# A filler tile that is 96 floats longer, and with it the addresses of every MLP operand

## The chip, the cores and the metric

The kernel runs on one core of one Trainium2 chip. The metric is the device time in microseconds (us) from the first to the last instruction's work, as the runtime sees it, for one execution of the whole layer; lower is better. The time before is 1979.04 us, the median of three runs (1976.56, 1979.04, 1983.78).

## What is computed

One layer of a decoder trunk, float32, sequence 2048, width 1024. The first part mixes tokens (attention beside a short convolution) and adds the result to the residual; the second part is an MLP with a squared ReLU. The filler stands between the two, and the MLP is the part whose operands it moves.

```
h  = rms_norm(x, attn_norm_g);  z = h @ w_in                  # 1024 -> 2304 columns
q, k, v, B, C, xc = split(z)
y  = [rms_norm(swa_sink_attention(q, k, v)), rms_norm(B * conv3(C * xc))]
x  = x + y @ w_out                                            # 1024 -> 1024
hm = rms_norm(x, mlp_norm_g)
x  = x + square(relu(hm @ w_up)) @ w_down                     # 1024 -> 4096 -> 1024
```

## The kernel before, in words

**Three stages.** The mixers run first, in four chunks of 512 tokens, each a sequence of projections (accumulators `pz`, `pc_c`, `px_c`, `pb_c`), attention (`psc_b`, `ptp_b`, `po_b`) and output projection (`pout`). Then comes the first MLP product, called "up" here (accumulators `u`, line 1222), and then the second, called "down" (accumulators `d`, line 1328). The matrices of the MLP are cut into 2x2 blocks and multiplied in seven block products instead of eight (a Strassen-like scheme), so that up is 224 products of 12 matmuls and down is 56 steps of 48, which makes 2688 matmuls in each.

**Every matmul is split in three.** To keep float32 accuracy with the PE's rounded operand type (fp32r), each operand is stored as a high part and a remainder: ScalarE (ACT) casts the block, VectorE (DVE) subtracts, and TensorE (PE) does high x high, high x low and low x high into one accumulator. In the mixers this is the helper at lines 245 to 247; in up and down it is the innermost loop. All of these matmuls have a stationary operand of 128x128 and, where the text speaks of a wide matmul, a moving operand of 128x512. In the profile's names the moving operand stands first: `u<-op_x,wop` moves `op_x` past a stationary `wop`, and `d<-op_w,op_f` moves `op_w` past `op_f`.

**Where the operands lie.** A tile's address is its byte in each partition of SBUF. Three pools matter. `mlp_ops`, on the right side of SBUF, has 14 buffers of 8192 bytes, tag `op`, for the moving operand of up (`op_x`), and both operands of down (`op_w`, `op_f`); and then, behind the last of them, the tile `fill`. Since this pool is laid out up to the end of SBUF, the length of `fill` sets where the 14 buffers begin. `mlp_up`, on the left side, holds the stationary operand of up (`wop`, four buffers of 4096 bytes) and the raw weights and intermediate results of up; `mlp_down` takes its place in the down stage. The mixers' pools are given back before `mlp_ops` and `mlp_up` are opened. Inside a tile the pieces that one matmul reads are at multiples of 512 bytes from its start (128 or 512 floats in a row), so a tile's start says where all of its pieces lie, counted modulo 512. In the program before these starts are:

```
stage    moving operand, start mod 512      stationary operand, start mod 512
mixers   w_wo, w_q, h            0          at_b, yt_c, h, w_wc, w_wx, w_wb   0
up       op_x                  384          wop                               0
down     op_w                  384          op_f                            384
```

**What sets the order.** The order of up's products is written out (`seq`); three products ahead of the PE, ACT and DVE make the next `wop` from raw weights `wu` (lines 963 and 964), and up's results go out to DRAM as the blocks `fop` (line 975). In the first part of up, between its products, sixteen groups of four PE transposes (`pt_m`, line 1050) prepare the second half of the tokens. Down loads `fop` back, splits it (lines 896 to 898), and forms the weights' sums on DVE (line 1176) from raw blocks that SP's queue loads (line 1167). `fill` itself is only written once, by a memset of GpSimd (POOL) at line 1202, and nothing reads it.

Of the kernel before, what the change touches and what calls it, by code (L numbers as in the profile page):

```python
# [7 lines left out]
F32 = mybir.dt.float32  # L8
# [8 lines left out]
P = 128  # L17
# [75 lines left out]
def hymba_layer(  # L93
# [794 lines left out]
    ops = ctx.enter_context(tc.tile_pool(name="mlp_ops", bufs=1, side="right", reuse_waits="tile"))  # L888
# [309 lines left out]

    ready_x(0)

    fill = ops.tile([P, 24], F32, tag="fill", name="fill")
    nc.gpsimd.memset(fill, 0.0)
    for i in range(LEAD):
        ready_x(i)
# [163 lines left out]
```

## Time and profile before

| | |
|---|---|
| profiled execution | 1980.8 us, of which 1978.8 us from first to last instruction (the span) |
| PE busy | 1945.1 us (98%) of the span |
| DVE, ACT, POOL busy | 1189.2, 837.2, 317.2 us (60%, 42%, 16%) |
| DMA | 410.66 MB, mean 208 GB/s |
| chain that ended last | PE 93%: up (L1222) 32%, down (L1328) 31%, the rest in the mixers |

The profile names an instruction by its line, engine, operation and tiles. PE means matmuls and PEld the weight loads that go before them. A matmul's own duration (about 390 ns) overlaps with the next one's, so what a matmul costs the PE in a dense stretch is the distance from its start to the next one's start; it comes from a stretch's length divided by the number of matmuls in it. "The chain" is the work that ended last, followed back from the end; a row of it gives the start, the length, the line and the number of instructions. PEclk is the granted TensorE clock as a share of full speed.

### The profile page before, as it was taken

The numbers are of one execution on the slowest core, as the hardware profiler recorded it, in microseconds if no ns is written. First come the engines' busy times: TensorE is split into PE (matmuls) and PEld (weight loads), VectorE is DVE, ScalarE is ACT, GpSimd is POOL, SyncE is SP. The second block draws the span as 40 slices with busy tenths as digits, with TensorE's granted clock in tenths as the row PEclk, the third lists the DMA queues.
The fourth block names the chain that finished last, engine by engine and source line by source line (L and its number), as shares of the span: only waits on it lengthen the run. The fifth ranks groups of instructions, "written<-read, shape, count | busy, mean of one in ns | idle before, by whom it ended". The sixth has DMA issues, their size and how long they took to land.

```text
span 1978.8 us, 24773 instructions
## 1 busy us (share of the span) xinstructions
PE 1945.1 (98%) x9068; PEld 1608.4 (81%) x9068; DVE 1189.2 (60%) x1810; ACT 837.2 (42%) x1572; POOL 317.2 (16%) x492
## 2 busy tenths in 40 slices
PE   8999999999999989999999999999999999999999
PEld 7878887888788768888888888888888888888887
DVE  4875656446555759777778766665643434547441
ACT  4474435335334446444455544454433232232320
POOL 2332314313132310222201111011000000100000
PEclk9999999999999999999999999999999999999999
DMA  8875744464464696666665444436974447766641
GB/s 286 295 295 160 293 181 163 169 256 181 150 261 186 211 295 244 214 212 194 232 221 199 164 156 143 150 114 225 411 254 143 145 149 229 273 224 218 214 149 43
DMA packets 224057, 410.66 MB, mean 208 GB/s; under 512 B 18368, under 2 KB 134080, under 8 KB 212160
## 3 DMA queue, kind: packets, MB, share of 16 engines
q1 hardware_dynamic: 195072, 333.57, 49.6%
q0 software_dynamic: 15040, 50.34, 6.6%
q10 hardware_dynamic: 13824, 25.17, 3.4%
q8 instruction: 71, 1.16, 0.2%
q14 instruction: 50, 0.41, 0.1%
HBM read 283.20 MB, written 125.83 MB: 207 GB/s over the span
## 4 chain that ended last, share of the span: by engine, by line
PE 93%; DVE 3%; POOL 1%; ACT 1%; DMA 1%; issue 1%; SPq 0%; DVEq 0%; POOLq 0%; ACTq 0%
PE u L1222 32%; PE d L1328 31%; PE pout L245 3%; PE pout L247 3%; PE pout L246 3%; PE pz L246 2%; PE pz L245 2%; PE pz L247 2%; PE psc_b L502 1%; PE pc_c L246 1%; PE pc_c L245 1%; PE pc_c L247 1%; PE px_c L245 1%; PE px_c L247 1%; PE px_c L246 1%; PE pb_c L247 1%
## 5 line engine op out<-in xcount | busy, mean ns | idle before, releaser
L1222 PE MATMUL u<-op_x,wop 128*128 128x512 f32 x2688 | 634.0, 397 | 4.6 <-ACT wop L963 4.5
L1328 PE MATMUL d<-op_w,op_f 128*128 128x512 f32 x2688 | 609.6, 389 | 0.0
L1222 PEld LDWEIGHTS u<-op_x,wop 128*128 128x128 f32 x2688 | 505.1, 188 | 126.8 <-ACT wop L963 5.7
L1328 PEld LDWEIGHTS d<-op_w,op_f 128*128 128x128 f32 x2688 | 504.5, 188 | 104.8
L898 DVE TENSOR_TENSOR op_f<-op_f 128x1024 fp32r<-128x1024 f32 x112 | 136.7, 1224 | 237.2 <-ACT op_f L897 237.1
L897 ACT CAST op_f<-op_f 128x1024 fp32r<-128x1024 f32 x112 | 117.4, 1050 | 330.1 <-DMA op_f<-fop 327.2
L963 ACT CAST wop<-wu 128x512 fp32r<-128x512 f32 x160 | 99.0, 619 | 124.4 <-PE u L1222 118.3
L964 DVE TENSOR_TENSOR wop<-wu,wop 128x512 fp32r<-128x512 f32 x160 | 110.2, 689 | 43.3 <-ACT wop L963 27.5
L975 POOL DMA_DIRECT2D fop<-s x96 | 52.1, 542 | 486.3 <-DVE s L978 464.3
L981 DVE TENSOR_TENSOR u<-u,u 128x512 f32<-128x512 f32 x128 | 88.1, 688 | 35.6 <-PE u L1222 33.9
L898 DVE TENSOR_TENSOR op_w<-raw,op_w 128x1024 fp32r<-128x1024 f32 x56 | 68.4, 1223 | 34.1 <-ACT op_w L897 33.9
L897 ACT CAST op_w<-raw 128x1024 fp32r<-128x1024 f32 x56 | 58.7, 1049 | 58.2 <-PE d L1328 29.3
L1178 POOL DMA_DIRECT2D wds<-raw x16 | 8.6, 534 | 335.6 <-DVE raw L1176 335.6
L519 ACT ACTIVATE sc_b<-sc_b,ngm_b 128x128 f32<-128x128 f32 x128 | 49.6, 389 | 27.4 <-DVE ngm_b L516 27.4
L551 POOL TENSOR_SCALAR_AFFINE_SELECT pp_b<-pp_b 128x512 fp32r<-128x512 f32 x60 | 42.7, 725 | 111.6 <-ACT pp_b L544 73.1
L963 ACT CAST wop<-wu_s 128x512 fp32r<-128x512 f32 x64 | 39.6, 619 | 44.2 <-PE u L1222 42.6
L987 ACT ACTIVATE u<-u 128x512 f32<-128x512 f32 x64 | 40.5, 633 | 33.9 <-DVE u L981 30.9
L245 PE MATMUL pout<-w_wo,yt_c 128*128 128x512 f32 x128 | 52.8, 412 | 0.0
L247 PE MATMUL pout<-w_wo,yt_c 128*128 128x512 f32 x128 | 52.5, 410 | 0.0
L246 PE MATMUL pout<-w_wo,yt_c 128*128 128x512 f32 x128 | 51.9, 406 | 0.0
L245 PE MATMUL pout<-w_wo,at_b 128*128 128x512 f32 x128 | 50.2, 392 | 0.0
L247 PE MATMUL pout<-w_wo,at_b 128*128 128x512 f32 x128 | 50.0, 391 | 0.0
(236 smaller groups left out, 3181.1 us busy)
## 6 DMA issues: line engine op xcount, KB each, us to landing
op_f<-fop SPq DMA_DIRECT2D x112, 512.0 KB, 3.8
raw<-in_w_down_dram SPq DMA_DIRECT2D x72, 512.0 KB, 4.3
wu<-in_w_up_dram SPq DMA_DIRECT2D x128, 256.0 KB, 3.6
w_wo<-wo SPq DMA_DIRECT2D x24, 1024.0 KB, 6.7
fop<-s POOLq DMA_DIRECT2D x96, 256.0 KB, 2.4
fop<-u ACTq DMA_DIRECT2D x64, 256.0 KB, 2.2
op_x<-xop SPq DMA_DIRECT2D x28, 512.0 KB, 5.8
w_q<-qkv SPq DMA_DIRECT2D x24, 512.0 KB, 5.4
```

The costliest lines, as they stand in the source:

```text
L245: nc.tensor.matmul(ps, st(0), mv(0), start=first, stop=False)
L246: nc.tensor.matmul(ps, st(0), mv(1), start=False, stop=False)
L247: nc.tensor.matmul(ps, st(1), mv(0), start=False, stop=last)
L519: nc.scalar.activation(sc[:, hd, :], sc[:, hd, :], AF.Exp, bias=ngm[:, hd : hd + 1], accum_out=den[:, hd : hd + 1])
L897: nc.scalar.copy(op[:, 0], raw)
L898: nc.vector.tensor_tensor(op[:, 1], raw, op[:, 0].bitcast(F32), op=ALU.subtract)
L963: nc.scalar.copy(hi, blk)
L964: nc.vector.tensor_tensor(lo, blk, hi.bitcast(F32), op=ALU.subtract)
L975: eng.dma_start(fop_dram[tb][ORDER_DOWN.index(i)][n // 2][:, n % 2], b)
L981: nc.vector.tensor_tensor(dst, ps, b, op=ALU.add)
L1222: nc.tensor.matmul(pt, wops[i][:, a, k, :], xops[tb, p][k // 2][:, b, k % 2, :], start=p not in GOES_ON and k + j == 0, stop=k + j == NB + ...
L1328: nc.tensor.matmul(ps[tb][j], fs[tb][:, a, k, j * P : (j + 1) * P], w[:, b, k, :], start=first and p not in GOES_ON and k + n == 0, stop=l ...
```

## The change

The filler grows from 24 to 120 floats in each partition, from 96 to 480 bytes.

```diff
-    fill = ops.tile([P, 24], F32, tag="fill", name="fill")
+    fill = ops.tile([P, 120], F32, tag="fill", name="fill")
     nc.gpsimd.memset(fill, 0.0)
```

In the built program one instruction differs, the memset, which now writes 120 elements of each partition; every other instruction, its place on its engine and its waits are the same, so there is no order to show. What moves is the address of the 14 `op` buffers, by 384 bytes downwards: the first starts at 114176 instead of 114560, which is 0 instead of 384 modulo 512. The nearest tile below them ends at 113152. So the table of starts becomes 0 and 0 in up and 0 and 0 in down; the mixers keep theirs.

## Rows read from the trace of the kernel before

**Rows 1.** The page: the granted TensorE clock in 40 slices of the span, in tenths of full speed, and the two MLP products among the costliest groups (busy us, mean ns of one | idle before).

```profile
PEclk9999999999999999999999999999999999999999
...
L1222 PE MATMUL u<-op_x,wop 128*128 128x512 f32 x2688 | 634.0, 397 | 4.6 <-ACT wop L963 4.5
L1328 PE MATMUL d<-op_w,op_f 128*128 128x512 f32 x2688 | 609.6, 389 | 0.0
```

**Rows 2.** The chain that ended last, from the start of up to the start of down, in two answers (start us, length us, what): the first rows of up, and the rest of up with the beginning of down.

```profile
729.93 74.34 PE u L1222 x310
804.27 0.44 PE pt_m L1050 x4
804.70 5.59 PE u L1222 x24
810.29 0.44 PE pt_m L1050 x4
810.73 5.60 PE u L1222 x24
...
961.96 0.44 PE pt_m L1050 x4
962.40 397.59 PE u L1222 x1704
1359.99 0.24 PE d L1328
1360.22 0.06 issue
1360.29 5.82 PE u L1222 x24
1366.10 34.03 PE d L1328 x150
```

**Rows 3.** Busy time by stretch for the matmuls of down alone (line 1328): the whole of the down stage.

```profile
core 0: us, PE busy (x) PEld busy (x), PEclk, DMA share, GB/s
...
1366.00:1975.00 609.00, 609.00 (x2687) 504.07 (x2686) 1.00 0.60 207
```

**Rows 4.** Busy time by stretch for the matmuls of up alone (line 1222).

```profile
740.00:800.00 60.00, 60.00 (x260) 48.66 (x259) 1.00 0.71 249
...
804.00:965.00 161.00, 157.92 (x662) 122.90 (x661) 1.00 0.64 205
965.00:1360.00 395.00, 394.99 (x1693) 317.43 (x1691) 1.00 0.51 172
```

**Rows 5.** Timeline of the PE in two settled stretches of the mixers, the first and the last matmul of each (start us, duration us). The first stretch has 80 wide matmuls, the second 82, one to a row.

```profile
213.04 0.39 PE L245 MATMUL pout<-w_wo,at_b 128*128 128x512 f32 x1
...
230.95 0.39 PE L246 MATMUL pc_c<-h_h,w_wc 128*128 128x512 f32 x1
...
390.42 0.39 PE L246 MATMUL pout<-w_wo,at_b 128*128 128x512 f32 x1
...
408.78 0.39 PE L246 MATMUL pc_c<-h_h,w_wc 128*128 128x512 f32 x1
```

**Rows 6.** Timeline of the PE in the mixers just behind an interruption by narrower matmuls.

```profile
252.38 2.08 PE L502 MATMUL psc_b<-kw,qt_b 128*128 128x256 f32 x16
254.29 0.40 PE L245 MATMUL px_c<-h_h,w_wx 128*128 128x512 f32 x1
254.53 0.40 PE L246 MATMUL px_c<-h_h,w_wx 128*128 128x512 f32 x1
254.76 0.39 PE L247 MATMUL px_c<-h_h,w_wx 128*128 128x512 f32 x1
254.99 0.40 PE L245 MATMUL px_c<-h_h,w_wx 128*128 128x512 f32 x1
255.22 0.39 PE L246 MATMUL px_c<-h_h,w_wx 128*128 128x512 f32 x1
255.46 0.39 PE L247 MATMUL px_c<-h_h,w_wx 128*128 128x512 f32 x1
```

**Rows 7.** Busy time by stretch of all engines, over up and, in the second part, over two settled stretches of the mixers.

```profile
core 0: us, PE busy (x) PEld busy (x) DVE busy (x) ACT busy (x) POOL busy (x), PEclk, DMA share, GB/s
729.00:804.00 75.00, 74.92 (x312) 60.11 (x312) 65.39 (x95) 46.00 (x70) 6.87 (x18) 0.96 0.77 266
804.00:965.00 161.00, 161.00 (x726) 130.24 (x725) 121.91 (x177) 76.32 (x127) 39.45 (x45) 1.00 0.64 205
965.00:1360.00 395.00, 395.00 (x1694) 317.62 (x1692) 284.86 (x421) 209.63 (x340) 47.53 (x86) 1.00 0.51 172
...
213.00:231.00 18.00, 18.00 (x81) 14.89 (x81) 11.47 (x22) 4.06 (x7) 9.14 (x14) 1.00 0.79 309
235.00:252.00 17.00, 17.00 (x77) 14.07 (x76) 8.45 (x17) 5.93 (x24) 0.18 (x1) 1.00 0.92 356
```

**Rows 8.** Waits: those of the PE over the whole of up (729 to 1366 us), then the longest of the other engines for the PE between 965 and 1360 us, then one of SP's queue between 1300 and 1420 us (who waited <- for whom: us in total, times, longest).

```profile
PE u L1222 <- ACT wop L963: 4.5, 1, 4.5
...
ACT wop L963 <- PE u L1222: 100.0, 78, 2.2
...
SPq L1167 <- DMA fop<-u: 21.1, 1, 21.1
```

**Rows 9.** Timeline of DVE where the third step of down gets its operand `op_f` (two blocks, one for each half of the tokens).

```profile
1385.77 2.35 DVE L898 TENSOR_TENSOR op_f<-op_f 128x1024 fp32r<-128x1024 f32 x2
```

**Rows 10.** The same work of DVE at either offset (mean ns of one behind the busy time): the split of `op_f`, at 384 modulo 512, and the difference of two raw weight blocks, at 0; and the DMA issues of 512 KB into `op_f` and into `raw_t` (x count, KB, median us to landing), with the same two offsets.

```profile
L898 DVE TENSOR_TENSOR op_f<-op_f 128x1024 fp32r<-128x1024 f32 x112 | 136.7, 1224 | 237.2 <-ACT op_f L897 237.1
...
L1176 DVE TENSOR_TENSOR raw<-raw,raw 128x1024 f32<-128x1024 f32 x16 | 19.6, 1222 | 13.6 <-DMA raw<-in_w_down_dram 13.5
...
op_f<-fop SPq DMA_DIRECT2D x112, 512.0 KB, 3.8
raw_t<-wds SPq DMA_DIRECT2D x16, 512.0 KB, 4.1
```

**Rows 11.** The memset of the filler (duration ns min/median/max, first and last start us).

```profile
L1202 POOL MEMSET fill<- x1: 118/118/118, 731.3 to 731.3; 128x24 f32 x1
```

## The prediction, made before the changed kernel ran

> **What bounds the kernel now.** I read the shares of busy time first, then the chain that ended last, then the spacing of the matmuls stretch by stretch, and only then the waits. The PE is busy for nearly all of the span and carries nearly all of the chain; up and down are about a third of it each. The groups of the page show the first thing that needs an explanation: up and down have the same number of matmuls of the same shape, 2688 of 128x512, and yet up keeps the PE busy for 634.0 us and down for 609.6 [rows 1].
>
> A difference like that could come from waits or from the clock, so both have to be looked at. In up the PE waited for another engine once, for 4.5 us at the very start [rows 8]. The granted clock is at its upper level, 2.4 GHz, from 740 us on: the stretches show 1.00 [rows 3, 4]. What is left is the spacing itself. Down runs 2687 matmuls in 609.00 us, which is 226.65 ns from start to start [rows 3]. Up, in its long undisturbed piece, runs 1704 in 397.59 us, which is 233.3 ns [rows 2], and the stretch from 965 to 1360 us says the same (394.99 us over 1693) [rows 4]. The short pieces between the transposes, 24 in 5.60 us, give 233.3 too [rows 2]. Before the first transposes the pace is a little better: 60.00 us hold 260 matmuls, but a stretch counts those that lie in it in part, and as one lasts 0.39 us there are about 1.7 of these, so 60.00 over 258.3 is 232.3 ns [rows 4].
>
> So the PE has two paces for one shape of matmul, and in neither does anything wait. Which pace belongs to what? The mixers answer that. They have wide matmuls in the same three-part form. Of those I take the settled stretches: from 213.04 to 230.95 us there are 79 steps from the first row to the last, 17.91 us, or 226.7 ns; from 390.42 to 408.78 us there are 81 in 18.36 us, 226.7 ns again [rows 5]. Set beside the table of starts: mixers, 0 and 0, fast; down, 384 and 384, fast; up, 384 and 0, slow. The pace goes with whether moving and stationary operand start at the same place modulo 512, not with whether each is a multiple of 512. The trace shows that coincidence, not what inside the chip makes it.
>
> Two other readings are excluded as far as the trace goes. It is not other engines' traffic: in one settled mixer stretch DVE is busy for 11.47 of 18.00 us and the DMA engines for 79%, in another the DMA share is 92%, and the pace is the fast one, while the slow stretch from 965 to 1360 us has DVE at 72% and DMA at 51% [rows 7]. And it is not the accumulation: `pout`, like a product of up, adds 12 matmuls into one accumulator, and it is fast [rows 5].
>
> **The change part by part.** First, the memset. It took 118 ns for 24 elements [rows 11]. For 120 I bound it between that and five times it, 0.6 us; POOL is busy for 6.87 of 75.00 us around it [rows 7] and nothing reads the filler, so on the path it costs nothing. Were POOL full it would cost its 0.6 us once.
>
> Second, the new addresses for down. Moving and stationary operand go from 384 and 384 to 0 and 0. They stay equal, and 0 and 0 is what the mixers have at the same 226.7 ns [rows 5], so the term is nothing. What it costs if that is wrong is the last rival below.
>
> Third, the new addresses for ACT, DVE and DMA, which write and read the same buffers. DVE took 1224 ns for a block at 384 and 1222 for one of the same shape at 0; 512 KB land in 3.8 us at 384 and in 4.1 at 0 [rows 10]. Nothing there depends on the offset by more than 0.3 us for a transfer that is issued well ahead of its use, so I take nothing.
>
> Fourth, up, where moving and stationary go from 384 and 0 to 0 and 0. If it takes the fast pace, each matmul gives back 233.3 - 226.65 = 6.68 ns, and in the first stretch 232.3 - 226.65 = 5.65. Of the 310 matmuls before the first transposes I leave out ten for the start, where the granted clock is lower (0.96 over that stretch) [rows 7]: 300 x 5.65 = 1.70 us. The pieces between the transposes are 2688 - 310 - 1704 - 24 = 650 matmuls: 650 x 6.68 = 4.34 us. The long piece and the last 24 [rows 2] are 1728 x 6.68 = 11.54 us. Together 17.58 us.
>
> From that something goes back. After an interruption the fast pace is not there at once, as the mixers show: behind the narrower matmuls at 252.38 us the next five steps take 255.46 - 254.29 = 1.17 us where five at the fast pace would take 1.13 [rows 6]. Sixteen groups of transposes stand in up, so 16 x 0.04 = 0.6 us stay. The transposes themselves, 0.44 us a group, are work and stay as well. The gain is 17.0 us; its bounds are nothing, if up keeps its pace, and 17.6, if there is no settling.
>
> **What the faster PE meets.** In up ACT waits for the PE to free a buffer (100.0 us in 78 waits), not the PE for ACT [rows 8]. DVE's share rises from 65.39 of 75.00 us (87%) to 65.39 of 73.3 (89%) in the first stretch and from 72% to 74% in the long one [rows 7], so no engine becomes the bound. The thinnest place is the third step of down: DVE finishes its first `op_f` at 1385.77 + 1.18 = 1386.95 us [rows 9]. The step begins after 96 matmuls; one of them ran at 1359.99 us, so its first is the 96th from 1366.10, at 1366.10 + 95 x 0.2267 = 1387.6 us [rows 2], and its weights load a matmul earlier, 0.4 us after the operand is ready. The raw weights for it hang off the end of up, since SP's queue waits 21.1 us for `fop<-u` to land [rows 8], and so move with up; I take nothing for this and allow up to 1 us.
>
> **The sum.** 1980.8 us, the profiled execution, less 17.0 is 1963.8. The median of the three runs lies 1.8 us below the profiled one, so the forecast for the median is 1962.0.
>
> A rule speaks against all this. The Trainium skill, "TensorE: Matmul & The Clock Gate", section "Step-by-step: what each phase is for", says that the PE has two independent read ports into SBUF, one for the streaming operand and one for the weights. By that rule where the one lies against the other would not matter, and the time would stay at 1979. The trace does not fit it easily, as up at 233.3 ns beside down at 226.65 shows, but no run so far has moved an address alone.
>
> **The rivals.** *No change* (about 1979 us): the slow pace belongs to something else that only up has, such as its stationary tile in the left pool behind its moving one in the right, and the addresses modulo 512 are a coincidence. For it: there are only three stages, and up differs from the others in more than offsets. Against it: the mixers too have a moving operand above its stationary one (`pc_c<-h_h,w_wc`, at 230.95 us) at 226.7 ns [rows 5], and every other cause that I could name has a fast stretch that shares it.
>
> *The supply cannot follow* (about 1969 us): up takes the fast pace but from 729 to 965 us, where DVE is busiest [rows 7], the PE waits for `wop` and keeps today's pace: 1.7 + 4.3 us are not won, and 1 us is lost at the third step of down. That leaves 17.0 - 7.0 = 10 us. It decides once DVE has more work than the shortened stretch is long; at 89% it has not.
>
> *Slower* (about 1997 us): a start at 0 is bad for buffers of this pool whatever the other operand does. Then up stays at 233.3 ns and down falls from 226.65 to that: 2688 x 6.68 = 18.0 us more. From 6.3 ns a matmul in down on (17.0 us over 2688) it would undo a full gain in up. The fast mixers at 0 and 0 [rows 5] speak against it; that they use other buffers is what leaves it open.
>
> **How the numbers follow.** I give the forecast 0.78, no change 0.12, the short supply 0.04 and slower 0.06. A difference under 0.5%, 9.9 us, I count as none, about what a measurement of this kernel can tell. Faster by more than that is the forecast and half of the short supply, 0.80; within it the other half and no change, 0.14; slower 0.06. The forecast's own range is 1958 to 1968: below, the bound of 17.6 us and a median as low as the fastest run (2.5 us under); above, 1 us at down's start and the slowest run (4.7 us over). To hold 8 in 10 the range has to take in the short supply as well, with the same spread above it: 1958 to 1973.
>
> **What would show it.** In the changed kernel's profile up's long piece should run at 226.7 ns (its 1704 matmuls in 386.2 us instead of 397.59), its group of the page should fall from 634.0 to about 617 us, down should stay at 609 us, and the mixers should keep their times. If up's pace stays at 233.3, the offset is not the cause; if it falls to something between, the relation of the addresses counts in more than steps of 512. If the pace is right and the time is not, the loss should stand among the PE's waits: for `wop`, or for `op_f` at down's start.

## The result, and the profile after

The changed kernel takes 1964.07 us (median of four runs, 1960.7 to 1968.55) where the kernel before takes 1980.84 (median of its four, 1976.56 to 1983.78). The ratio is 0.9918 with a 95% interval of 0.989 to 0.9947, so it is faster by 10 to 22 us; 17.0 were forecast.

The page of the changed kernel, its span and the two groups that [rows 1] shows of before:

```profile
span 1966.9 us, 24773 instructions
...
L1222 PE MATMUL u<-op_x,wop 128*128 128x512 f32 x2688 | 617.8, 391 | 7.2 <-ACT wop L963 6.4
L1328 PE MATMUL d<-op_w,op_f 128*128 128x512 f32 x2688 | 609.6, 389 | 0.0
```

Up's busy time is down by 16.2 us, from 634.0, and down's is the same to the tenth. The chain of the changed kernel, from the start of up to the start of down, in two answers (start us, length us, what), stands against [rows 2]:

```profile
725.89 6.91 DMA wu<-in_w_up_dram
733.49 72.92 PE u L1222 x310
806.85 5.50 PE u L1222 x24
...
961.16 376.79 PE u L1222 x1662
1337.97 4.81 DMA op_f<-fop
...
1342.80 1.05 ACT op_f L897
1343.86 0.52 ACT wop L963
1344.37 0.53 ACT u L987
1344.90 0.95 ACT op_f L897
...
1345.94 1.08 issue
1347.02 0.68 DVE s L978
1347.70 0.61 DVE u L981
...
1348.45 5.73 PE u L1222 x24
1354.18 46.01 PE d L1328 x203
```

The long piece now runs 1662 matmuls in 376.79 us, 226.7 ns each where it was 233.3. Behind it the chain does not go on with PE as before: it goes over to a load of `op_f`, ScalarE's casts and VectorE before the last 24 matmuls of up. That ends in a new wait, and the waits of the PE from 733 to 1360 us say how long it is:

```profile
PE u L1222 <- DVE u L981: 0.8, 1, 0.8
PE u L1222 <- ACT wop L963: 0.7, 1, 0.7
```

The first row is the new wait. The second is the end of the wait for the first `wop` at up's start, at 733.49 us.

The same stretches as in [rows 4], with the end cut at 1335 us to stay ahead of that wait:

```profile
core 0: us, PE busy (x) PEld busy (x), PEclk, DMA share, GB/s
740.00:800.00 60.00, 60.00 (x266) 49.67 (x266) 1.00 0.74 254
...
965.00:1335.00 370.00, 370.00 (x1634) 306.39 (x1633) 1.00 0.51 174
```

Before the transposes 60 us hold 266 matmuls instead of 260, that is 60.00 over 264.3, or 227.0 ns. The long stretch gives 370.00 over 1632.3, or 226.7 ns. The granted clock is 1.00 as it was.

**Why this profile's span fell by only 11.9 us.** Up began 3.56 us later than in the profile before (733.49 against 729.93), behind mixers that have the same instructions at the same addresses: the load of `wu` started 1.72 us later (725.89 against 724.17) and took 6.91 us where it had taken 5.06. From up's start to down's first full stretch it is 1354.18 - 733.49 = 620.7 us against 1366.10 - 729.93 = 636.2, a gain of 15.5. The start of up differs from one profile to the next without any reason in the change (728.79 us in the first experiment below, 725.69 in the third). Between profiled executions at the same pace it is most of the difference: the changed kernel's took 1968.55 us, the first experiment's 1962.82, and up began 4.70 us apart. The pace of a stretch does not have that spread.

### The profile page after: what moved, and what is told of

Its sections match the earlier page's. It is cut to its first block, busy times and chain, and to the rows that moved or that the text cites. A ratio compares the mean times of both kernels' runs of the same rounds, so it can differ in the third digit from the quotient of the medians.

```text
span 1966.9 us, 24773 instructions
## 1 busy us (share of the span) xinstructions
PE 1930.4 (98%) x9068; PEld 1610.1 (82%) x9068; DVE 1189.0 (60%) x1810; ACT 836.5 (43%) x1572; POOL 316.2 (16%) x492
## 4 chain that ended last, share of the span: by engine, by line
PE 91%; DVE 3%; DMA 2%; ACT 2%; POOL 1%; issue 1%; SPq 0%; DVEq 0%; ACTq 0%; POOLq 0%
PE d L1328 31%; PE u L1222 31%; PE pout L247 3%; PE pout L245 3%; PE pout L246 3%; PE pz L246 2%; PE pz L245 2%; PE pz L247 2%; PE psc_b L502 1%; PE pc_c L246 1%; PE pc_c L245 1%; PE pc_c L247 1%; PE px_c L245 1%; PE px_c L247 1%; PE px_c L246 1%; PE pb_c L247 1%
## 5 line engine op out<-in xcount | busy, mean ns | idle before, releaser
L1222 PE MATMUL u<-op_x,wop 128*128 128x512 f32 x2688 | 617.8, 391 | 7.2 <-ACT wop L963 6.4
L1328 PE MATMUL d<-op_w,op_f 128*128 128x512 f32 x2688 | 609.6, 389 | 0.0
L898 DVE TENSOR_TENSOR op_w<-raw,op_w 128x1024 fp32r<-128x1024 f32 x56 | 68.4, 1222 | 35.0 <-ACT op_w L897 35.0
```

The costliest lines, as they stand in the source:

```text
L898: nc.vector.tensor_tensor(op[:, 1], raw, op[:, 0].bitcast(F32), op=ALU.subtract)
L1222: nc.tensor.matmul(pt, wops[i][:, a, k, :], xops[tb, p][k // 2][:, b, k % 2, :], start=p not in GOES_ON and k + j == 0, stop=k + j == NB + ...
L1328: nc.tensor.matmul(ps[tb][j], fs[tb][:, a, k, j * P : (j + 1) * P], w[:, b, k, :], start=first and p not in GOES_ON and k + n == 0, stop=l ...
```

## The experiments

The theory from the prediction is that the slow pace comes when moving and stationary operand of a wide matmul start at different places modulo 512 bytes. The rivals are that each operand has to lie at a multiple of 512, and that the pace belongs to something else of up. The experiments move addresses alone: all eleven profiles have 24773 instructions, and no edit touches an engine's order of work. Those that move an address inside a tile of down read other columns of it, in the same amount. "Distance" below is the start of the stationary operand less that of the moving one; the profile's rows are read as above (length over number of matmuls, in a stretch after taking 1.7 off the number).

**Equal, but no multiple of 512.** The kernel before, with the left side behind the tile `pad` (the buffers of the mixers and of up) moved by 384 bytes:

```diff
-    small.tile([P, 16], F32, name="pad")
+    small.tile([P, 112], F32, name="pad")
```

> The kernel before, with the filler of before, and with the unused pad tile of the left side 96 floats longer, so that every buffer of the mixers and of the left MLP pool starts at 384 modulo 512, where the op buffers lie already. Moving and stationary operands then start at equal offsets in all three stages, and none at a multiple of 512. If equal offsets make the fast pace: up's long piece of 1704 matmuls at 226.7 ns in place of 233.3, mixers and down as before, time about 1964 us (as after). If multiples of 512 make it: up at 233.3 ns or more, the mixers slower than 226.7 in their settled stretches, time 1981 us or more. If the pace belongs to something else of up: 1981 us with the mixers unchanged.

It took 1961.3 us, ratio to before 0.9901 (0.9887 to 0.9916). The chain's long piece of up:

```profile
955.23 371.35 PE u L1222 x1638
```

That is 226.7 ns with the short filler and not one operand of up at a multiple of 512. A settled stretch of the mixers, now at 384 and 384, keeps the fast pace too: 71 steps from 212.63 to 228.73 us, 226.8 ns. The gain does not come from the multiple, and up has nothing else that makes it slow.

**The old distance with the new filler.** The same longer pad in the changed kernel, so that the op buffers lie at 0 and `wop` at 384:

> The changed kernel (long filler, op buffers at 0 modulo 512) with the same longer pad on the left, so that up moves an operand at 0 past a stationary one at 384: the difference of before with its sign turned. Equal offsets: up slow again, about 233 ns, while down (0 and 0) and mixers (384 and 384) are fast, time about 1981 us. Multiple of 512 for the op buffers alone: up stays at 226.7 ns, 1964 us. Multiples of 512 for both: up slow and the mixers slow too, over 1981 us.

It took 1978.06 us, ratio 0.9981 (0.997 to 0.9992). Up's long piece and, below it, a stretch of down in the chain:

```profile
961.93 395.98 PE u L1222 x1704
...
1365.84 607.25 PE d L1328 x2679
```

Up is slow again, 232.4 ns, and down, with both at 0, runs at 226.7. The new filler alone wins 0.9 ns a matmul in up's long piece, 232.4 for 233.3, and not the 6.6 of the change.

**A distance of 256.** The kernel before with a filler of 56 floats (`fill = ops.tile([P, 56], ...)`), which puts the op buffers at 256 and leaves `wop` at 0:

> The kernel before with a filler of 56 floats: op buffers at 256 modulo 512, wop at 0. If only equality modulo 512 counts, up's long piece stays slow, 230 ns or more (time about 1975 to 1985 us). If equality modulo 256 is enough, it runs at 226.7 ns (about 1964 us). Down, 256 and 256, at 226.7 ns by either.

One run, 1959.55 us; up's long piece:

```profile
952.45 367.27 PE u L1222 x1620
```

226.7 ns. Equality modulo 256 bytes is enough, so the prediction's 512 was too coarse.

**The narrow transposes.** The changed kernel with the identity matrix moved from 128 to 0 modulo 512:

```diff
-    small.tile([P, 16], F32, name="pad")
+    small.tile([P, 48], F32, name="pad")
...
-    ident = const.tile([P, P], F32, name="ident")
+    const.tile([P, 96], F32, name="ident_pad"); ident = const.tile([P, P], F32, name="ident")
```

> The changed kernel with the identity matrix moved from 128 to 0 modulo 512 (all of the left side by 512 bytes, so that everything else keeps its offset). It is the moving operand of all PE transposes; their stationary operands lie at 0. If unequal offsets slow the narrow transposes as they slowed up, by 3% or so of their 109 ns over some 500 transposes, 1.5 us are won, 1962.5 us; if they are bound by something else, 1964 us as the changed kernel. Up stays at 226.7 ns either way.

1964.97 us, ratio 0.9918 (0.9904 to 0.9931), the same as the changed kernel. The two largest groups of transposes, first in the changed kernel and then here:

```profile
L538 PE MATMUL ptp_b<-ident,sc_b 128*128 128x128 f32 x128 | 28.3, 274 | 0.0
...
L1050 PE MATMUL pt_m<-ident,xt_m 128*128 128x128 f32 x64 | 9.6, 271 | 0.0
```

```profile
L538 PE MATMUL ptp_b<-ident,sc_b 128*128 128x128 f32 x128 | 28.0, 272 | 0.0
...
L1050 PE MATMUL pt_m<-ident,xt_m 128*128 128x128 f32 x64 | 9.6, 271 | 0.0
```

No difference that could be told: the second group is the same, and of the first's 0.3 us nothing belongs to the distance, since the third experiment, which leaves the transposes' operands where they were, has 28.0 us too. Their distance of -128 costs these transposes nothing that shows, and the extra 1.5 us were not there.

**The same in down.** The changed kernel, whose down stage reads its stationary operand 128 bytes further on:

```diff
+    def shifted(f, at):
+        at -= P if at + P > 4 * BW else 0
+        return f.rearrange("p a k c -> p (a k c)")[:, at : at + P]
...
-                            fs[tb][:, a, k, j * P : (j + 1) * P],
+                            shifted(fs[tb], (2 * a + k) * BW + j * P + 32),
```

> The changed kernel, in which down reads its stationary operand 32 floats (128 bytes) further on in the tile; the numbers that it multiplies are then the wrong columns, the amount of work is the same. Up keeps 0 and 0, down has 0 moving and 128 stationary. If unequal starts make the slow pace wherever they stand, down takes 230 to 235 ns a matmul in place of 226.65, 9 to 22 us more over 2688, so about 1973 to 1986 us; if the slow pace was something of up's, down stays at 226.65 and the time at 1964.

1981.24 us, ratio to before 1.001 (0.9999 to 1.0022): all of the gain is gone. The chain's piece for down and, in a second answer, up's long piece:

```profile
1344.73 624.42 PE d L1332 x2687
```

```profile
952.29 378.15 PE u L1222 x1668
```

Down runs at 232.4 ns in place of 226.65, and up keeps 226.7. The slow pace can be given to either stage by distance alone.

**Which distances.** The same edit with another shift in each of down's seven products, in two kernels (`{5: 0, 3: 32, 1: 16, 2: 8, 6: 4, 7: 48, 4: 64}[p]` floats in place of 32, then `{5: 1, 3: 12, 1: 24, 2: 40, 6: 52, 7: 56, 4: 60}[p]`):

> The same with another shift in each of down's seven products, in floats: 0 for product 5, 32 for 3, 16 for 1, 8 for 2, 4 for 6, 48 for 7, 64 for 4 (0, 128, 64, 32, 16, 192 and 256 bytes); the columns multiplied are wrong again. If equality modulo 256 bytes is what counts, products 5 and 4 run at 226.65 ns and all others slower; if only some distances collide, those near 128 (3, perhaps 7) are slow and the small shifts fast; if equality modulo 512 counted after all, 4 would be slow too.

> The changed kernel with shifts of down's stationary operand that the first map left out (again the wrong columns are multiplied): product 5 by 4 bytes, 3 by 48, 1 by 96, 2 by 160, 6 by 208, 7 by 224, 4 by 240. If only equality modulo 256 bytes gives 226.67 ns, all seven are slower, by 2 ns or more. If the cost falls off towards a whole 256 from below (192 cost 2.2 ns where 64 cost 6.7), the products with 208, 224 and 240 bytes lie between 228.9 and 226.67 and fall in that order, and 5, 3 and 1 are near 233.

They took 1976.73 and 1977.3 us, one run each. A stretch of 80 us out of each product, in the order 5, 3, 1, 2, 6, 7, 4 (matmuls of down alone), first the first kernel and then the second:

```profile
1355.00:1435.00 80.00, 80.00 (x354) 66.25 (x353) 1.00 0.95 364
1440.00:1520.00 80.00, 80.00 (x346) 64.83 (x345) 1.00 0.50 171
1530.00:1610.00 80.00, 80.00 (x344) 64.48 (x343) 1.00 0.43 140
1620.00:1700.00 80.00, 80.00 (x344) 64.39 (x344) 1.00 0.72 234
1710.00:1790.00 80.00, 80.00 (x345) 64.78 (x344) 1.00 0.64 223
1800.00:1880.00 80.00, 80.00 (x351) 65.63 (x350) 1.00 0.67 231
1887.00:1967.00 80.00, 80.00 (x355) 66.26 (x354) 1.00 0.18 61
```

```profile
1350.00:1430.00 80.00, 80.00 (x346) 64.52 (x346) 1.00 0.92 355
1440.00:1520.00 80.00, 80.00 (x344) 65.11 (x343) 1.00 0.50 168
1530.00:1610.00 80.00, 80.00 (x343) 64.29 (x343) 1.00 0.44 143
1620.00:1700.00 80.00, 80.00 (x344) 64.38 (x343) 1.00 0.73 237
1710.00:1790.00 80.00, 80.00 (x346) 64.73 (x346) 1.00 0.63 216
1800.00:1880.00 80.00, 80.00 (x344) 64.26 (x343) 1.00 0.69 232
1887.00:1967.00 80.00, 80.00 (x352) 65.73 (x351) 1.00 0.18 60
```

At distances 0 and 256 bytes 354 and 355 matmuls fit into 80 us, which is the fast pace (80 over 352.3 is 227.1 ns, over 353.3 it is 226.4). Every other distance holds fewer: 343 to 346 (232.4 to 234.4 ns) at 4, 16, 32, 48, 64, 96, 128, 160, 208 and 224 bytes, 351 at 192 and 352 at 240 (229.0 and 228.4 ns); one matmul more or less in a count is 0.7 ns. Product 4 of the first kernel reads shifted columns like the slow ones and is fast, so it is the distance that slows them and not the shifted reading. The second expectation's order does not come out: 192 is cheaper than 208 and 224, so the cost does not fall off smoothly towards 256. And it is not traffic: the stretch with the highest DMA share of the first kernel, 0.95, is a fast one, and the stretch of product 1 with 0.43 is slow. At 240 bytes the cost is 1.7 ns, a little less than the 2 ns that the expectation set as the least.

**Two more fillers.** The kernel before with 104 and with 88 floats, so that up has a distance of -64 (192 modulo 256) and of -128:

> The kernel before with a filler of 104 floats: op buffers at 64 modulo 512, wop at 0. Equality modulo 256: up slow, 229 ns or more, time 1968 to 1985 us. Only some distances collide: up at 226.7 ns, 1964 us. It should agree with product 1 or 7 of the map.

> The kernel before with a filler of 88 floats: op buffers at 128 modulo 512, wop at 0, the same distance modulo 256 as before. Equality modulo 256: up at about 233 ns, 1980 us, as before. If 384 as such were bad and not its distance: up at 226.7 ns, 1964 us.

1966.18 and 1981.13 us, one run each; up's long pieces, one answer each:

```profile
955.00 381.80 PE u L1222 x1668
```

```profile
962.49 382.20 PE u L1222 x1638
```

These are 228.9 and 233.3 ns. The first, with its 1966.18 us, lies just under the slow range that was expected (229 ns, 1968 us). It is the pace that 192 bytes gave in down, where 64 gave 233.7 (344 in 80 us): at this distance the map holds for up too, and the sign counts. The second is the pace of before.

## Why the prediction was right

**The two paces.** Right, and in its size: 6.68 ns a matmul in the long piece were expected back and 6.6 came (233.3 to 226.7). Up's group fell to 617.8 us where about 617 were forecast, and down stayed at 609.6. That the pace goes with where the two operands lie to one another, and with neither address alone, is shown by the first two experiments and by down's shift, each of which moves nothing but addresses. The step of the prediction that was wrong is the period: not 512 bytes but 256. For this change it made no difference, since 0 and 0 is equal by both.

**What goes back.** The settling behind the transposes was sized at 0.6 us in all. A piece of 24 now takes 5.50 us where 24 at 226.65 would take 5.44; that is 0.06 a group, 1.0 us for sixteen, so this term was too small by 0.4 us.

**What the faster PE meets.** The prediction looked for the thin place at down's third step and allowed 1 us there. The PE did not wait in down at all. It waited 0.8 us just ahead of the last 24 matmuls of up, and the chain above shows for what: ScalarE casts two blocks of `op_f` for down, one of them 1.05 us long, VectorE comes to up's own sums behind them, and the PE waits for that sum. Of the eight profiles with a faster up seven have such a wait, 0.3 to 0.8 us long; of the three at the old pace (before, the second experiment and the last) only the last has one, 0.2 us. So the effect was of the right size and at another place. The loads of `op_f` do not come at a time of their own: SP's queue issues them when the PE frees their buffers, and the wait for that moves with the PE. The first of these loads, and two of up's sums on VectorE, of which the last 24 matmuls need the first, before and then after (start us, duration us):

```profile
SPq L896 <- PE u L1222: 51.3, 4, 42.5
1340.42 0.34 SPq L896 DMA_DIRECT2D op_f<-fop  x1
1359.46 1.48 DVE L981 TENSOR_TENSOR u<-u,u 128x512 f32<-128x512 f32 x2
```

```profile
SPq L896 <- PE u L1222: 49.2, 4, 40.9
1328.45 0.34 SPq L896 DMA_DIRECT2D op_f<-fop  x1
1347.62 1.48 DVE L981 TENSOR_TENSOR u<-u,u 128x512 f32<-128x512 f32 x2
```

From the load's start to the sums' it is 19.0 us before and 19.2 after. The PE came to its last 24 matmuls 19.8 us behind the load before (1360.22, [rows 2]) and 19.2 after (1348.45 less the wait of 0.77). So before it came just behind the sum, and now the faster pace over these 19 us brings it there ahead of the sum.

**The sum.** 17.0 us were forecast and the medians differ by 16.8; of the profile's terms, 16.2 in up's busy time less 0.8 of the new wait make 15.4, and the 15.5 from the chain agree. By the chain, the first 310 matmuls gave back 1.4 us (1.7 were summed), the stretch of the transposes 3.4 (4.3 less 0.6), and the rest of up 10.7 (11.5), 0.8 of the shortfall being the new wait. So the mechanism is worth about 1.5 us less than the forecast, and that the medians come within 0.2 us of it is luck: their interval is 10 to 22 us.

**The rivals.** *No change* is out: the second experiment has a slow up (232.4 ns) with all else new, the first has the new pace with the old filler. *Short supply* did not come: between up's start and its last 24 matmuls the PE waited for nothing, and the 0.8 us at the end are a wait for a sum and not for `wop`. *Slower* is out, as down kept 226.7 ns at 0 and 0; down slows to 232.4 only when its own two operands are set apart.

**The rule that spoke against it.** By the Trainium skill, "TensorE: Matmul & The Clock Gate", section "Step-by-step: what each phase is for", the streaming operand and the weights come through two independent read ports. The measurement decides otherwise for these matmuls: with equal instructions, and addresses alone moved, the distance of the two operands adds 1.7 to 7.7 ns to the 226.7. That the two reads get in each other's way is one reading of this; what in the chip does it no run here shows.

## What to carry to other kernels

If two stretches of equal matmuls have different start-to-start times and neither waits, look at the addresses of their operands before looking for a busy engine: here the distance of stationary to moving operand modulo 256 bytes decided 3% of the pace. For matmuls like these, a filler or pad that makes that distance a whole multiple of 256 is enough; aligning each operand is not needed, and an alignment of one alone can win next to nothing. Read the pace from long dense pieces of the chain, where 0.1 ns shows, and not from the span, whose start of a stage moves by several us from one execution to the next.

## What the runs showed of the hardware that was not expected

- The wide matmul (128x512, a weight load before each) settles at 226.7 ns at the distances of 0 and 256 bytes (modulo 512) that were tried, and at 228.4 to 234.4 ns at the twelve other distances (modulo 256) that were tried. A single element, 4 bytes, costs as much as 128 bytes.
- One distance can have two paces: 128 modulo 256 gave 233.3 ns in up's long piece before and 232.3 in its first stretch [rows 4], and 232.4 with the sign turned and in down. In the second experiment the two stretches of up have changed places. The chain from 740 to 800 us has 259 matmuls in 60.19 us before (232.4 ns) and 258 in 60.20 in that experiment (233.3), where the long pieces have 233.3 and 232.4. What chooses between the two paces was not found.
- Matmuls with a moving operand of 128 columns, the transposes, showed no cost of a distance of -128 (28.0 us for 128 of them at -128 in the third experiment and at 0 in the fourth). Other widths and other types were not tried.
